# Bursts of small fp32 products split among dense matmuls in a two-layer delta-rule encoder, and the inverse placed three chunks later

## The chip, the cores and the metric

The kernel runs on one core of a Trainium2 chip. The metric is the time of one execution on the device in microseconds (us); shown are the median and the extremes of three executions. The trace is of one further execution, recorded by the hardware profiler, with its own time.

## The reference: what is computed

Two encoder layers work on 1040 tokens (1024 and 16 meta tokens) of width 1024. Per layer: RMS norm; one input projection, whose columns feed a gated delta rule in both directions (4 heads of 128) and a gated short convolution (4 groups of 128 channels); an output projection of both, added to the residual; RMS norm, a SwiGLU feed-forward, and a second residual. A last norm ends it. The part that the change touches is the delta rule, cut to its core:

```python
A = M + jnp.eye(CHUNK)                      # M strictly triangular, from keys, decay, beta
u = triangular_solve(A, vb, lower=True, unit_diagonal=True)
w = triangular_solve(A, kb * exp(G), lower=True, unit_diagonal=True)
def step(S, inp):                           # over the chunks of tokens
    v_new = u_c - w_c @ S
    o = qd_c @ S + attn_c @ v_new
    S = S * gl_c + kd_c.T @ v_new
```

It runs once forward and once backward over the tokens. The kernel solves with the inverse of A.

## The kernel before, in words

**Dense work.** `dense` (L156) is every large product. Operands are kept as a high and a low part (`whi`, `wlo` of the weights; the tiles `a`, `b` hold those of the input). For each chunk of columns (346, 346 and 348 of 1040, or 512 and 512 in the last layer's halves) and each of 8 slices of the contraction, it issues three matmuls: hi·hi (L169), hi·lo (L170), lo·hi (L171), 24 in all for a projection of 1024 rows. After each chunk's evacuation one job is taken from each of three lists, `jobs`, `jobs2`, `jobs3` (L183). An entry None lets one chunk pass.

**Order.** Engines take their instructions in the order that a scheduler writes down at build time: by priorities, and by a simulated timeline. `low(f, True)` emits a set of matmuls as one burst and ties its first to the last dense matmul emitted, so that a burst stands behind the chunk after which its job was taken. A matmul of 32x32 fp32 operands shows as two matmuls and two weight loads in the trace.

**The inverse.** The delta rule uses chunks of 128 tokens: 8 chunks by 4 heads by 2 directions gives 64 triangular matrices, 32 per direction, kept in the tiles P (`Pd[0]` forward, `Pd[1]` backward, named `P0` and `P1`). Their 32x32 diagonal blocks are inverted on VectorE by substitution (operations on `e` at L613 and `b` at L614 move blocks into matmul layout). `invert` (L606) then builds the rest from products of blocks, as jobs of the third list: `first` (L639, 128 calls of 32x32, 256 matmuls in the trace), `second_third` for each half of the matrices (L651 and L652, 96 calls, 192 matmuls), `fourth` (L675) and `fifth` (L695), 64 calls of 64x64 each, 128 matmuls. Evacuations on ScalarE and VectorE stand between the steps. The list before is seven None, then `first`, None, `second_third` twice, None, `fourth`, None, `fifth`. Products of keys and queries, `chunk_a` (L573), are jobs of the second list in the same stretch.

**The scan.** After `fifth` the scan starts: eight steps for each direction, forward and backward side by side, with products at L926 (keys or queries by state, inverse by residual, attention and keys by new values) and small ones of the meta tokens at L1004. Each step loads V (`vkd`), K (`vkd`) and the attention (`aqd`) into tile `rec`, which takes the place in SBUF of the inverse's working tile (`W` and `X`), so those loads wait until the inverse has read it for the last time. Transposes of the result are at L1071. While the scan runs, TensorE's gaps are filled with dense matmuls: the rest of the input projection, then the half of the output projection that takes the convolution's rows y (four rows; loaded at L1105, split at L1110 and L1111). The other half of it takes the delta rule's result O, split at L1138 and L1139, and can only start behind the scan.

**Places in SBUF.** The third y row (i = 2) is loaded into tile P1, the place of the backward inverse. The residual rows are loaded into `hb[0]` and `hb[1]` (L1127, eight of them), which take the places of tiles of the input projection's operand x in that layer.

All these loads are issued by SyncE (SP) in one list, in order.

## Time and profile before

| | |
|---|---|
| median of 3 executions | 2438.77 us (2432.99 to 2439.55) |
| the profiled execution's own time | 2442.37 us |
| its span, first to last instruction | 2440.6 us |
| mean granted TensorE clock | 0.995 |
| busy: PE, PEld, DVE, ACT, POOL | 2410.2, 2235.0, 1824.9, 1053.0, 68.5 us |
| inverse's matmuls, layer 0 / layer 1 | about 244 to 287 us / 1464 to 1518 us of the span |

PE is TensorE's matmuls, PEld its weight loads, which overlap them. A row of the timeline has the start, the duration, the engine, the line and the operation with its tiles and shape, a count (x), and in brackets the idle time before it with what released it; "issue" is time in which the engine waited for nothing that the profile shows. A row of a windows view gives, after the bounds and the length, the busy time and number of instructions of PE, PEld, DVE, ACT and POOL, then the granted clock of TensorE as a share of full speed, the share of DMA engines in use, and GB/s.

### The profile page before, as it was taken

What the parts mean: (1) busy time and instruction counts of PE and PEld (TensorE: products, weight loads), DVE (VectorE), ACT (ScalarE), POOL (GpSimd) and SP (SyncE); (2) the same over time, 40 slices, a digit from 0 to 9 for tenths busy, and PEclk for the clock granted to TensorE, in tenths of its full rate; (3) what the DMA queues carried; (4) which work ended last, traced back from release to release, by engine and by line L of the source; (5) the groups of instructions that cost most, each with busy time, mean ns of one, the idle gap of its engine ahead of it and who ended that gap; (6) DMA issues with size and microseconds to landing.
All of it is one profiled execution on the core that took longest, in us unless ns stands there. A gap on an engine that the chain in (4) does not pass through costs nothing.

```text
span 2440.6 us, 44951 instructions
## 1 busy us (share of the span) xinstructions
PE 2410.2 (99%) x17559; PEld 2235.0 (92%) x17559; DVE 1824.9 (75%) x3312; ACT 1053.0 (43%) x1985; POOL 68.5 (3%) x157
## 2 busy tenths in 40 slices
PE   9999899999999999999999999999999999999998
PEld 8989899999999999999999998999988888888887
DVE  6778546668888887878657885457698887878874
ACT  6652434436233433344446624345453333334444
POOL 0130000000000000000000200000000000000002
PEclk9999999999999999999999999999999999999999
DMA  4456344534222224675224553445333222347641
GB/s 135 149 160 200 108 152 149 177 111 143 101 79 101 96 79 138 215 235 160 80 90 141 175 183 127 144 148 199 123 120 109 86 104 90 122 137 248 201 132 70
DMA packets 202637, 336.60 MB, mean 138 GB/s; under 512 B 23488, under 2 KB 89208, under 8 KB 202424
## 3 DMA queue, kind: packets, MB, share of 16 engines
q1 hardware_dynamic: 174600, 295.12, 36.4%
q10 hardware_dynamic: 25648, 34.24, 4.4%
q0 software_dynamic: 2176, 4.36, 0.6%
q8 instruction: 138, 2.26, 0.4%
q14 instruction: 75, 0.61, 0.1%
HBM read 251.52 MB, written 82.12 MB: 137 GB/s over the span
## 4 chain that ended last, share of the span: by engine, by line
PE 89%; DMA 4%; DVE 3%; ACT 1%; issue 1%; SPq 0%; ACTq 0%; DVEq 0%; POOLq 0%
PE pacc L170 9%; PE pacc L169 9%; PE pacc L171 9%; PE pacc L1226 4%; PE pacc L1230 4%; PE pacc L1229 4%; PE pb L1230 3%; PE pb L1226 3%; PE pb L1229 3%; PE pf L926 3%; PE pf L1226 3%; PE pf L1230 3%; PE pf L1229 3%; PE pb L926 3%; PE pacc L1793 2%; PE pacc L1794 2%
## 5 line engine op out<-in xcount | busy, mean ns | idle before, releaser
L169 PE MATMUL pacc<-a,whi 128*128 128x346 f32 (+1 forms) x800 | 261.0, 327 | 0.7 <-ACT a L190 0.6
L171 PE MATMUL pacc<-a,wlo 128*128 128x346 f32 (+1 forms) x800 | 261.1, 327 | 0.4 <-DVE wlo L139 0.2
L171 PE MATMUL pacc<-b,wlo 128*128 128x346 f32 (+2 forms) x672 | 232.3, 346 | 1.5 <-DVE wlo L139 1.3
L169 PE MATMUL pacc<-b,whi 128*128 128x346 f32 (+2 forms) x672 | 233.2, 348 | 0.0
L170 PE MATMUL pacc<-a,whi 128*128 128x346 f32 (+1 forms) x681 | 222.8, 327 | 0.5 <-DVE a L191 0.4
L138 ACT ACTIVATE whi<-raw 128x512 fp32r<-128x512 f32 x166 | 104.5, 632 | 238.3 <-PE pacc L170 169.5
L170 PE MATMUL pacc<-b,whi 128*128 128x346 f32 (+2 forms) x580 | 200.2, 345 | 0.0
L169 PEld LDWEIGHTS pacc<-a,whi 128*128 128x128 f32 x800 | 152.2, 190 | 1.8 <-ACT a L190 1.3
L171 PEld LDWEIGHTS pacc<-a,wlo 128*128 128x128 f32 x800 | 152.0, 190 | 2.0 <-DVE wlo L139 1.1
L139 DVE TENSOR_TENSOR wlo<-raw,whi 128x512 fp32r<-128x512 f32 x166 | 113.9, 687 | 48.8 <-ACT whi L138 44.3
L171 PEld LDWEIGHTS pacc<-b,wlo 128*128 128x128 f32 x672 | 126.8, 189 | 12.1 <-DVE wlo L139 1.9
L169 PEld LDWEIGHTS pacc<-b,whi 128*128 128x128 f32 x672 | 126.8, 189 | 10.3 <-issue 1.5
L170 PEld LDWEIGHTS pacc<-a,whi 128*128 128x128 f32 x681 | 129.6, 190 | 4.9 <-issue 2.5
L170 PEld LDWEIGHTS pacc<-b,whi 128*128 128x128 f32 x580 | 109.5, 189 | 7.1 <-issue 0.6
L1208 ACT ACTIVATE whi<-rw 128x512 fp32r<-128x512 f32 (+1 forms) x84 | 51.7, 620 | 105.9 <-PE pacc L1229 28.3
L1208 ACT ACTIVATE b<-rw 128x512 fp32r<-128x512 f32 (+1 forms) x63 | 38.8, 620 | 90.2 <-PE pb L1229 35.0
L1208 ACT ACTIVATE a<-rw 128x512 fp32r<-128x512 f32 (+1 forms) x63 | 38.5, 619 | 72.0 <-PE pacc L1229 33.2
L1209 DVE TENSOR_TENSOR wlo<-rw,whi 128x512 fp32r<-128x512 f32 (+1 forms) x84 | 56.2, 672 | 6.3 <-ACT whi L1208 5.8
L333 DVE TENSOR_TENSOR a<-pacc,rstd 128x346 f32<-128x346 f32 (+2 forms) x59 | 32.6, 553 | 36.3 <-PE pacc L171 36.1
L1794 PE MATMUL pacc<-P,wlo 128*128 128x260 f32 (+1 forms) x177 | 59.4, 336 | 0.0
L1791 PE MATMUL pacc<-P,whi 128*128 128x260 f32 (+1 forms) x177 | 59.4, 336 | 0.0
L1793 PE MATMUL pacc<-P,whi 128*128 128x260 f32 (+1 forms) x177 | 59.4, 336 | 0.0
(1163 smaller groups left out, 7851.0 us busy)
## 6 DMA issues: line engine op xcount, KB each, us to landing
raw<-in_w_in SPq DMA_DIRECT2D x110, 256.0 KB, 2.9
raw<-in_w_gu SPq DMA_DIRECT2D x106, 256.0 KB, 2.6
rw<-in_w_gu SPq DMA_DIRECT2D x90, 256.0 KB, 3.1
rw<-in_w_dn SPq DMA_DIRECT2D x90, 192.0 KB, 3.4
rec<-vkd SPq DMA_DIRECT2D x61, 256.0 KB, 3.2
raw<-in_w_out SPq DMA_DIRECT2D x48, 256.0 KB, 2.8
b<-ad SPq DMA_DIRECT2D x45, 260.0 KB, 3.9
a<-ad SPq DMA_DIRECT2D x45, 256.0 KB, 2.6
```

Of the source, the lines that this page charges most:

```text
L138: whi_done[0] = hasten(wpr, lambda: act(out=hi, in_=raw[:, 0:kk, :], func=AF.Copy))
L139: whi_done[1] = hasten(wpr, lambda: tt(out=lo, in0=raw[:, 0:kk, :], in1=hi.bitcast(F32), op=ALU.subtract))
L169: mm(ps[:, :n], wh, xh[:, n0:n1], start=(i == 0), stop=False)
L170: mm(ps[:, :n], wh, xl[:, n0:n1], start=False, stop=False)
L171: last_mm[0] = mm(ps[:, :n], wl, xh[:, n0:n1], start=False, stop=(i == K - 1))
L926: one = mm(*args, **kw)
L1208: hasten(wpr, lambda: act(out=hi, in_=src, func=AF.Copy))
L1226: one = mm(ps[:, :CW], w[0][:, k, :], th[:, cs], start=first and k == 0, stop=False, skip_group_check=True)
L1229: mm(ps[:, :CW], w[0][:, k, :], tl[:, cs], start=False, stop=False, skip_group_check=True)
L1230: one = mm(ps[:, :CW], w[1][:, k, :], th[:, cs], start=False, stop=stop and k == nk - 1, skip_group_check=True)
L1793: mm(ps[:, :CW], wh[:, k, :], tl[:, cs], start=False, stop=False, skip_group_check=True)
L1794: mm(ps[:, :CW], wl[:, k, :], th[:, cs], start=False, stop=en, skip_group_check=True)
```

## The change

`first` becomes two jobs of 64 calls (128 matmuls in the trace) and each `second_third` two jobs of 48 calls (96 matmuls); PSUM banks are kept between the parts of a step, and evacuations follow the last part. So between two bursts a chunk of dense matmuls passes. The list starts with ten None instead of seven. The first job therefore comes three chunks later; the four that are added move all that follows, `fifth` and the scan among it, later still. Since P1 is then still read by the scan when the third y row is loaded, that row goes into a row of `hb[1]` in the last layer. Numbers of lines are ten higher in the changed kernel from the middle of `invert` on.

```diff
-            def first():
-                pss = [view(bank("f"), 32) for _ in halves]
+            banks_ = {}
+            def first(part):
+                if part == 0:
+                    banks_["1"] = [view(bank("f"), 32) for _ in halves]
+                pss = banks_["1"]
...
-                low(lambda: [turn(q) for q in range(16)][0][0], True)
-                act(out=QS[:, halves[0], :], in_=pss[0], func=AF.Copy, scale=-1.0)
...
+                low(lambda: [turn(q) for q in range(8 * part, 8 * part + 8)][0][0], True)
+                if part == 1:
+                    act(out=QS[:, halves[0], :], in_=pss[0], func=AF.Copy, scale=-1.0)
...
-            def second_third(qs):
-                ps2, ps3 = (view(bank(t), 32) for t in "bf")
+            def second_third(qs, part):
+                if part == 0:
+                    banks_["2"] = [view(bank(t), 32) for t in "bf"]
+                ps2, ps3 = banks_["2"]
...
-                low(lambda: [turn(q) for q in range(qs.start, qs.stop)][0][0], True)
+                low(lambda: [turn(q) for q in range(qs.start + 8 * part, qs.start + 8 * part + 8)][0][0], True)
+                if part == 0:
+                    return
...
-            return [first, None, lambda: second_third(halves[0]), lambda: second_third(halves[1]), None, fourth, None, fifth]
+            return ([lambda i=i: first(i) for i in range(2)] + [None] + [lambda qs=qs, i=i: second_third(qs, i) for qs in halves for i in range(2)]
+                    + [None, fourth, None, fifth])
...
-                jobs3.extend([None] * 7 + invert())
+                jobs3.extend([None] * 10 + invert())
...
-            t = trow() if i < 2 else big("P1")[:, 0, :] if i < 3 else y3
+            t = trow() if i < 2 else (hb[1][:, i, :] if last else big("P1")[:, 0, :]) if i < 3 else y3
```

No instruction is added or taken away on any engine; they stand in another order between the inverse and the end of the scan, in both layers. Three places show it. A row is a line, an operation, the tile written and the tiles read, and the shape (x2: two alike in a row).

The first is PE around `first` in layer 0, where `pf` is the bank of the products, `pacc` that of a dense chunk. Before:

```order
L169 MATMUL pacc_2690<-a_1_72,whi_2467 128x346
L639 MATMUL pf_2557<-e_2163,P_836 32x32 x2
L639 MATMUL pf_2558<-e_2163,P_836 32x32 x2
L170 MATMUL pacc_2690<-a_2_73,whi_2467 128x346
...
L639 MATMUL pf_2558<-e_2164,P_837 32x32 x2
L171 MATMUL pacc_2690<-a_3_74,wlo_2474 128x346
L573 MATMUL pb_2716<-b_38_213,b_39_214 128x128 x4
L169 MATMUL pacc_2746<-a_1_72,whi_2734 128x348
```

and in the changed kernel:

```order
L171 MATMUL pacc_2639<-a_3_74,wlo_2608 128x346
L643 MATMUL pf_2665<-e_2163,P_836 32x32 x2
...
L643 MATMUL pf_2666<-e_2164,P_837 32x32 x2
L171 MATMUL pacc_2731<-a_1_72,wlo_2602 128x346
L169 MATMUL pacc_2731<-a_1_72,whi_2601 128x346
...
L171 MATMUL pacc_2731<-a_3_74,wlo_2608 128x346
L643 MATMUL pf_2665<-e_2163,P_836 32x32 x2
...
L643 MATMUL pf_2666<-e_2164,P_837 32x32 x2
L169 MATMUL pacc_2839<-a_1_72,whi_2827 128x348
```

Before, four calls stand ahead, then 13 dense matmuls, then 124 calls in one stretch. In the changed kernel 64 calls, 19 dense matmuls, and 64 calls follow each other.

The second is PE at the end of the scan in layer 1, `vv` being the scan's new values and `o` the split O. Before:

```order
L169 MATMUL pacc_18714<-b_1824_18680,whi_18708 128x512
L926 MATMUL pf_17895<-vv_17892,P_14797 128x128 x4
L170 MATMUL pacc_18714<-b3f_18690,whi_18708 128x512
...
L171 MATMUL pacc_18728<-b_1824_18680,wlo_18709 128x512
L926 MATMUL pf_17895<-vv_17892,rec_17887 128x128 x4
L169 MATMUL pacc_18749<-b_1824_18680,whi_18743 128x512
```

and in the changed kernel:

```order
L171 MATMUL pacc_18937<-b_1824_18680,wlo_18918 128x512
L936 MATMUL pf_17895<-vv_17892,P_14797 128x128 x4
...
L171 MATMUL pacc_18972<-b_1824_18680,wlo_18953 128x512
L936 MATMUL pf_17895<-vv_17892,rec_17887 128x128 x4
L169 MATMUL pacc_18972<-b_1824_18680,whi_18952 128x512
...
L171 MATMUL pacc_18972<-b_1824_18680,wlo_18953 128x512
L169 MATMUL pacc_19030<-o_18986,whi_19024 128x256
```

Before, 171 dense matmuls of the y half stand between the scan's last product and the first that reads `o`; in the changed kernel six.

The third is SP's list in the same stretch, with the y rows (`yd`), the residual rows (`hd`) and the scan's loads. Before:

```order
L1105 DMA P_1829_18687<-yd_14188 128x1024
...
L1105 DMA a_1825_18681<-yd_14188 128x1024
...
L1105 DMA a_1827_18684<-yd_14188 128x1024
L916 DMA rec_17887<-aqd_14190 128x512
...
L1127 DMA b_1823_18679<-hd_206 128x1024
L1127 DMA b_1822_18678<-hd_206 128x1024 x4
L1127 DMA b_1823_18679<-hd_206 128x1024 x3
```

and in the changed kernel:

```order
L925 DMA rec_17887<-vkd_14189 128x512 x2
L926 DMA rec_17887<-aqd_14190 128x512
L1115 DMA b_1823_18679<-yd_14188 128x1024
L1137 DMA b_1822_18678<-hd_206 128x1024 x4
L1137 DMA b_1823_18679<-hd_206 128x1024 x3
...
L1137 DMA b_1823_18679<-hd_206 128x1024
L923 DMA rec_17887<-vkd_14189 128x512 x2
```

The third y row moved from the front of the three to behind them, into `hb[1]` (the tile `b_1823`); the residual rows, which before came behind the scan's last V and attention loads, now stand ahead of several of them.

## The prediction

> **What bounds the kernel now.** I read the page first, then TensorE's waits, then its timeline where those waits stand. The page says that TensorE is the bound:

> ```profile
> PE 2410.2 (99%) x17559; PEld 2235.0 (92%) x17559; DVE 1824.9 (75%) x3312; ACT 1053.0 (43%) x1985; POOL 68.5 (3%) x157
> q8 instruction: 138, 2.26, 0.4%
> ```

> The span is 2440.6 us, so PE idles for 30.4 us in all, and an edit that only moves work can gain no more than part of those, plus whatever makes its busy time too long. The view of waits of PE names those of this stretch (total, times, longest):

> ```profile
> PE pf L639 <- issue: 3.9, 2, 2.0
> PE pb L651 <- issue: 2.5, 1, 2.5
> PE pf L639 <- DVE e L613: 1.8, 3, 1.2
> ```

> Three are waits for nothing that the profile shows. The timeline puts each inside a burst of 32x32 products:

> ```profile
> 243.88 1.52 PE L639 MATMUL pf<-e,P 32*32 32x32 f32 x157 [1.19 <-DVE e L613]
> 247.37 1.10 PE L639 MATMUL pf<-e,P 32*32 32x32 f32 x91 [1.97 <-issue]
> 264.75 0.27 PE L651 MATMUL pb<-P,b 32*32 32x32 f32 x3 [2.54 <-issue]
> 1464.38 1.45 PE L639 MATMUL pf<-e,P 32*32 32x32 f32 x148 [0.43 <-DVE e L613]
> 1467.79 1.09 PE L639 MATMUL pf<-e,P 32*32 32x32 f32 x104 [1.95 <-issue]
> ```

> What are they? One view gives the number of instructions from stall to stall (PE and PEld are both PE's instructions):

> ```profile
> 247.37:264.75 17.38, 14.84 (x511) 14.20 (x511) 13.55 (x19) 8.35 (x11) 0.00 (x0) 0.90 0.27 94
> 264.75:1467.78 1203.03, 1195.13 (x9540) 1175.82 (x9539) 902.43 (x1699) 510.19 (x988) 19.45 (x51) 1.00 0.41 136
> ```

> In the first stretch 511 + 511 = 1022 instructions, with two semaphore instructions in PE's list 1024 = 4 x 256. In the page, 2 x 17559 = 35118 PE instructions meet 138 packets on the instruction queue q8, 2.26 MB or 16 KB each: one for about 254. So I read the stalls as PE out of instructions at the edge of a block of 256, its next 16 KB not yet there. Between 247.37 and 264.75 a 256-block takes 4.3 us on average; in a burst, 1.1 us for 91 calls' matmuls and loads is 182 instructions, or 1.5 us per block. Over the whole span it is 2440.6 / 138 = 17.7 us a block. A fetch that takes more than 1.5 us and less than 17.7 us is hidden in dense work, and bare in a burst that covers a whole block.

> [...]

> Behind each stall comes a second cost. Windows of 3.41 us around them, with the granted clock third from the end:

> ```profile
> 244.27:247.68 3.41, 1.44 (x162) 1.34 (x159) 3.41 (x5) 3.37 (x4) 0.00 (x0) 1.00 0.07 26
> 247.68:251.09 3.41, 3.41 (x81) 3.35 (x70) 3.07 (x5) 3.34 (x4) 0.00 (x0) 0.50 0.60 212
> 261.33:264.74 3.41, 0.88 (x105) 0.79 (x94) 0.33 (x1) 0.40 (x1) 0.00 (x0) 1.00 0.03 5
> 264.74:268.16 3.42, 3.41 (x31) 3.34 (x31) 2.75 (x4) 0.59 (x1) 0.00 (x0) 0.50 0.02 5
> 1466.24:1469.65 3.41, 1.86 (x108) 1.69 (x109) 3.41 (x7) 3.34 (x5) 0.00 (x0) 1.00 0.41 153
> 1469.65:1473.06 3.41, 3.41 (x10) 2.63 (x9) 3.21 (x6) 3.36 (x4) 0.00 (x0) 0.50 0.86 299
> 1471.27 0.63 PE L170 MATMUL pacc<-b,whi 128*128 128x512 f32 x1
> 1471.70 0.63 PE L171 MATMUL pacc<-b,wlo 128*128 128x512 f32 x1
> 1478.77 0.40 PE L171 MATMUL pacc<-b,wlo 128*128 128x512 f32 x1
> 1479.01 0.40 PE L169 MATMUL pacc<-b,whi 128*128 128x512 f32 x1
> ```

> A window with PE busy for 0.88, 1.44 or 1.86 of 3.41 us is followed by one at half clock, in which dense matmuls start 0.43 us apart instead of 0.24.

> **The change part by part.** *The stalls.* Now 128 matmuls (256 with their loads) are the longest burst of 32x32, in `first`; 96 in `second_third`. In the changed order I counted instructions in blocks of 256, taking the layer's block edges from the stalls above. The blocks that hold the first bursts have 51 or more of their 256 in dense matmuls, those of `second_third` 63 or more, and before each block stand 38 dense instructions or more. A dense matmul with its load takes 0.16 us in narrow chunks (the steps of 272.29 and 272.45 below, and 4.0 us for 25), so 24 to 48 of them are 3.8 to 7.7 us. The shorter is still longer than any of the three stalls, and the fetch has also the 1.5 us of the block's own instructions. The gain is 1.97 + 2.54 + 1.95 = 6.4 us. Bounds: 0 and 6.4, the second being taken because the nearest row, the first `second_third` burst, with dense work ahead of it, runs 192 matmuls without any stall:

> ```profile
> 254.46:256.58 2.12, 2.12 (x195) 1.85 (x193) 2.12 (x3) 0.26 (x1) 0.00 (x0) 1.00 0.60 209
> ```

> *The half-clock windows.* The loss of one is what its matmuls would have taken less at full clock. With dense matmuls of 512 columns all through it, as in the last of the three, that is 3.41 x (1 - 0.24 / 0.43) = 1.5 us. The first two also hold small products and short idle times, which the clock touches less, and I take 1.35 for each: 4.2 us together, with bounds of 0 and 4.5. I take 4.2, since a window of the changed order would hold at most two bursts of 0.8 to 1.5 us and no idle time, which is nearest to the row at 254.46 with its clock of 1.00.

> *The wait for e.* Each `first` started before VectorE had its operands: 1.8 us. It now starts three chunks later; by the orders, 54 narrow matmuls (8.6 us) later in layer 0 and 74 wide ones (17 us) in layer 1. Both exceed the longest wait, 1.2 us, so 1.8 us goes. Bounds 0 and 1.8.

> *The scan's first loads.* They wait for `fifth`, since `rec` takes the inverse's place.

> ```profile
> 292.24 1.13 PE L926 MATMUL pb<-rec,P 128*128 128x128 f32 x8 [1.41 <-DMA rec<-vkd]
> 1522.82 0.42 PE L1004 MATMUL pf<-rec,Z 16*32 16x128 f32 x8 [0.91 <-DMA rec<-vkd]
> ```

> The order has 25 narrow dense matmuls between `fifth` and the scan in layer 0, before and now: the 1.4 us stay. In layer 1 it was 25 narrow ones (4.0 us) and is now 23 of 512 columns (23 x 0.235 = 5.4 us), 1.4 us more than before and so more than 0.91: that goes. Bounds 0 and 0.9.

> *More switches.* Where other products stand between dense ones, PE loses time at the change:

> ```profile
> 272.29 0.32 PE L169 MATMUL pacc<-a,whi 128*128 128x348 f32 x1
> 272.45 0.32 PE L170 MATMUL pacc<-a,whi 128*128 128x348 f32 x1
> 272.70 0.33 PE L675 MATMUL pb<-b,P 64*64 64x64 f32 x2
> 272.95 0.43 PE L171 MATMUL pacc<-a,wlo 128*128 128x348 f32 x1
> 273.22 0.32 PE L169 MATMUL pacc<-a,whi 128*128 128x348 f32 x1
> ```

> From 272.45 to 273.22 are two dense steps, 2 x 0.16 us, and 0.45 us for one small group. The orders have 245 such places in the stretch before, 248 now: 3 x 0.45 = 1.35 us. (The splits add more; smaller scan groups that now merge take some back.)

> *The third y row.* It is loaded into x's low half, so only after the last in-projection matmul; call that T.

> ```profile
> 1692.26 1.05 PE L926 MATMUL pf<-vv,rec 128*128 128x128 f32 x8
> ad<-b SPq DMA_DIRECT2D x20, 512.0 KB, 2.7
> b<-ad SPq DMA_DIRECT2D x4, 520.0 KB, 4.6
> b<-hd SPq DMA_DIRECT2D x8, 512.0 KB, 8.4
> rec<-vkd SPq DMA_DIRECT2D x61, 256.0 KB, 3.2
> L1110 ACT ACTIVATE b<-a x6: 613/616/618, 1682.0 to 1694.3; 128x512 fp32r<-128x512 f32 x6
> ```

> On PE then come 12 matmuls of the y half that need only the first rows (12 x 0.235 = 2.8 us) and, by the order, 19 products of the scan, 38 matmuls in the trace: at 0.8 us for eight, since 0.25 of the 1.05 us overlap what follows, 3.8 us, of which I count 3.5. That is 6.3 us. The load needs 2.7 to 8.4 us to land, the split 0.62 us on ScalarE: a wait of 0 to 2.7 us. Nearest is the 4.6 us of a load of this size into the same kind of tile, so I take 0. Behind that split on ScalarE stand the scan's own copies, which PE's next scan group waits for; on SP the eight residual rows and the last loads of the scan stand behind the load. Where the row is late, those are late next.

> *The scan's end in layer 1.* Before, the last scan product, at 1692.26, stood well ahead of O's use:

> ```profile
> 1733.59 0.28 PE L169 MATMUL pacc<-o,whi 128*128 128x256 f32 x1
> L1138 ACT ACTIVATE o<-a x16: 400/402/418, 1690.6 to 1714.7; 128x256 fp32r<-128x256 f32 x16
> 1686.48 4.46 SPq L1127 DMA_DIRECT2D b<-hd  x8
> ```

> 41 us of dense work lay between; now six matmuls, 1.4 us, and the scan's steps still have about 25 wide matmuls (5.8 us) between links. O's first product needs only the middle chunks of tokens, whose last transposes stand a few steps earlier; one product of the split takes 0.40 us on ScalarE and about as long on VectorE. I cost it at 0. The cover is those 5.8 us; without it, each us by which the scan is late is a us of the total, up to the price in the third rival. In layer 0 the scan still ends 111 dense matmuls ahead, 17 us: 0.

> *Sum.* 6.4 + 4.2 + 1.8 + 0.9 - 1.35 = 11.95 us. The profiled execution took 2442.37, so it would take 2430.4. The median of the runs is 3.6 us below that execution, so I predict 2438.8 - 11.9 = 2427 us.

> **The rivals.** *The clock stays.* The stalls go, but a half-clock window comes at each change of phase anyway, as each burst of small products leaves weak activity. For: the small products all remain, and the windows quoted show a stall and a burst together, so the rows can't part the two. Against: the `second_third` burst at 254.46 has 2.12 us of small products and a granted clock of 1.00 in the window that holds it. 4.2 us less gain: 2431. [...]

> *Stalls at new places.* `fifth` in layer 0 and `fourth` in layer 1 now fill 244 and 245 of a 256-block. The nearest row is a burst of the 64x64 kind that takes 2.27 us:

> ```profile
> 284.32:286.59 2.27, 2.27 (x131) 1.99 (x129) 1.46 (x3) 1.97 (x3) 0.00 (x0) 1.00 0.37 116
> ```

> If a fetch starts only as the block before it is entered and takes 3.4 to 3.9 us (2.5 us of stall and 1.1 to 1.5 us of burst), each stalls for 1.1 to 1.6 us, and a half-clock window of 1.3 us may follow: 5 to 6 us back, 2433. Against: 84 or more dense instructions stand ahead of each.

> *The scan's end is late: slower.* On SP nine loads of 512 KB (the third y row and the residual rows) now wait for T, and the V loads of the scan's next steps stand behind them. By the order, 105 wide matmuls of the y half stand between T and the product that needs that V: 105 x 0.235 = 24.7 us. If the nine go together as in the row above, V lands 4.46 + 8.4 us behind T, and its own 3.2 us after these: 16 us, in time. If they go one behind the other at the 2.7 or the 4.6 us of the single rows, that is 24 or 41 us, and 27 or 45 with V: PE waits 3 to 20 us, and since the y half runs out with the scan, all of it goes to the end. 2427 + 20 = 2447. The change turns slower from where V lands 19 us behind its need, 44 us behind T. For: the eight are issued in 4.46 us and share the same engines. Against: in the same row they land after 8.4 us, not eight times that of one.

> *It doesn't do it.* The order shows dense matmuls between all bursts, so the split is real; but if the stalls are no fetches, they come again, at 2438 to 2440.

> **How the numbers follow.** The forecast has 0.58, the clock 0.17, new stalls 0.10, the late end 0.08, no effect 0.07. A change under 0.3% (7.3 us) is about what this kernel's measurement can't tell from none, so faster means below 2431.5. That holds for 0.9 of the forecast, half of the clock's case and a fifth of the new stalls: 0.52 + 0.09 + 0.02 = 0.63. Slower means above 2446: 0.06, most of it the late end. The rest, 0.31, is no difference. The likeliest's own range is 2422 to 2432 (all terms at the ends nearest to them, and the spread of the runs); for 8 in 10 I take 2420 to 2438, which holds the first three cases.

> **What would show it.** Right: no idle time released by issue within L643, L658 or L659; a granted clock of 1.00 in all windows of the inverse; no wait for e at `first`; the wait for `rec` left only in layer 0; PE running without a gap from T through the first product that reads `o`. Wrong: idle time of 1 us or more inside `fourth` or `fifth`; half-clock windows behind a burst with no stall; PE waiting for the third y row, for `rec` or for `o` in layer 1's tail. More than 19 us of such waits there would make it slower.

## The result, and the profile after

The changed kernel took 2427.06 us (median of four, 2424.01 to 2428.56) against 2438.2 (four, 2432.99 to 2439.55): a ratio of 0.9957, 95% interval 0.9939 to 0.9975. Run again later, beside three other kernels on one chip, it took 2428.47 us (five) against 2441.14 (nine): 0.9944, 0.9931 to 0.9958. The forecast was 2427. That the number was met so closely is partly luck, as the terms below show: two were wrong in opposite directions.

The busy times on the page of the profile after:

```profile
PE 2403.6 (99%) x17559; PEld 2227.7 (92%) x17559; DVE 1823.3 (75%) x3312; ACT 1054.4 (43%) x1985; POOL 68.2 (3%) x157
```

and its waits of PE (total, times, longest):

```profile
PE pacc L169 <- DVE b L870: 2.1, 1, 2.1
...
PE pb L573 <- DVE dt L577: 0.8, 1, 0.8
...
PE pb L936 <- DMA rec<-vkd: 0.2, 1, 0.2
```

There is as much to do as before, in 2426.3 us of span instead of 2440.6. The waits for issue, for e, and nearly all for `rec` are gone; a wait of 2.1 us for an evacuation on VectorE (L870 is L860 of before) is new. To see where the time came from, the two stages that the change touches are cut out by counting dense matmuls: from the 1000th to the 2250th that starts, and from the 4000th to the 5250th. Before:

```profile
212.13:516.51 304.38, 296.69 (x2908) 291.52 (x2906) 187.54 (x399) 116.22 (x316) 0.00 (x0) 0.99 0.46 155
1447.33:1764.11 316.78, 313.46 (x2837) 289.18 (x2837) 200.41 (x399) 129.42 (x329) 0.00 (x0) 0.99 0.48 156
```

and after:

```profile
208.97:505.51 296.54, 294.21 (x2906) 288.57 (x2906) 187.64 (x400) 115.96 (x316) 0.00 (x0) 1.00 0.48 159
1436.47:1750.60 314.13, 312.87 (x2839) 287.83 (x2838) 199.41 (x398) 130.42 (x329) 0.00 (x0) 1.00 0.47 156
```

Layer 0's stage is 7.8 us shorter, layer 1's 2.7: 10.5 of the 14.3 us between the two spans. The other 3.8 us lie outside the stages, most of them where the two kernels have the same work in the same order. The profiled execution of before had half-clock windows (3.41 us with a granted clock of 0.50) at 56.5 and 138.5 us and the one of after had none there, so nothing shows these 3.8 us to be a gain of the change.

The bursts themselves, in a windows view of after (`first` twice, one part of `second_third`, `fourth` and `fifth` of layer 1, then each layer's whole inverse):

```profile
250.73:252.02 1.29, 1.29 (x130) 1.25 (x129) 1.13 (x2) 0.00 (x0) 0.00 (x0) 1.00 0.00 0
255.14:256.43 1.29, 1.29 (x130) 1.25 (x129) 1.29 (x2) 0.66 (x2) 0.00 (x0) 1.00 0.00 2
264.18:265.20 1.02, 1.02 (x98) 0.98 (x97) 0.52 (x1) 0.00 (x0) 0.00 (x0) 1.00 0.00 0
1515.44:1517.54 2.10, 2.10 (x130) 2.03 (x129) 0.52 (x1) 0.88 (x2) 0.00 (x0) 1.00 0.00 0
1527.03:1529.12 2.09, 2.09 (x130) 2.02 (x129) 0.97 (x2) 0.88 (x2) 0.00 (x0) 1.00 0.03 8
244.00:330.00 86.00, 85.80 (x1382) 82.23 (x1383) 45.65 (x76) 34.19 (x65) 0.00 (x0) 1.00 0.35 117
1455.00:1540.00 85.00, 83.74 (x1273) 72.39 (x1272) 47.19 (x67) 30.25 (x48) 0.00 (x0) 1.00 0.33 112
```

PE is busy through each burst, and the granted clock is 1.00 through both inverses.

### The profile page after: what moved, and what is told of

Its sections match the earlier page's. It is cut to its first block, busy times and chain, and to the rows that moved or that the text cites. A ratio compares the mean times of both kernels' runs of the same rounds, so it can differ in the third digit from the quotient of the medians.

```text
span 2426.3 us, 44950 instructions
## 1 busy us (share of the span) xinstructions
PE 2403.6 (99%) x17559; PEld 2227.7 (92%) x17559; DVE 1823.3 (75%) x3312; ACT 1054.4 (43%) x1985; POOL 68.2 (3%) x157
## 3 DMA queue, kind: packets, MB, share of 16 engines
q8 instruction: 138, 2.26, 0.4%
## 4 chain that ended last, share of the span: by engine, by line
PE 90%; DMA 4%; DVE 4%; ACT 1%; issue 1%; ACTq 0%; SPq 0%; DVEq 0%; POOLq 0%
PE pacc L169 9%; PE pacc L170 9%; PE pacc L171 9%; PE pacc L1236 4%; PE pacc L1240 4%; PE pacc L1239 4%; PE pb L1240 3%; PE pb L1236 3%; PE pb L1239 3%; PE pf L936 3%; PE pb L936 3%; PE pf L1236 3%; PE pf L1240 3%; PE pf L1239 3%; PE pacc L1804 2%; PE pacc L1803 2%
## 5 line engine op out<-in xcount | busy, mean ns | idle before, releaser
L169 PE MATMUL pacc<-a,whi 128*128 128x346 f32 (+1 forms) x800 | 259.7, 325 | 2.5 <-DVE b L870 2.1
L171 PE MATMUL pacc<-a,wlo 128*128 128x346 f32 (+1 forms) x800 | 259.0, 325 | 0.0
L169 PE MATMUL pacc<-b,whi 128*128 128x346 f32 (+2 forms) x672 | 233.6, 348 | 0.5 <-DVE a L870 0.5
L171 PE MATMUL pacc<-b,wlo 128*128 128x346 f32 (+2 forms) x672 | 231.4, 345 | 1.8 <-DVE wlo L139 1.7
L170 PE MATMUL pacc<-a,whi 128*128 128x346 f32 (+1 forms) x681 | 221.3, 325 | 0.4 <-DVE a L191 0.4
L170 PE MATMUL pacc<-b,whi 128*128 128x346 f32 (+2 forms) x580 | 199.2, 344 | 0.0
L169 PEld LDWEIGHTS pacc<-a,whi 128*128 128x128 f32 x800 | 150.8, 189 | 3.9 <-DVE b L870 2.4
L171 PEld LDWEIGHTS pacc<-a,wlo 128*128 128x128 f32 x800 | 150.4, 188 | 1.3 <-issue 0.9
L171 PEld LDWEIGHTS pacc<-b,wlo 128*128 128x128 f32 x672 | 126.4, 188 | 12.1 <-DVE wlo L139 2.3
L169 PEld LDWEIGHTS pacc<-b,whi 128*128 128x128 f32 x672 | 126.4, 188 | 10.8 <-issue 1.5
L170 PEld LDWEIGHTS pacc<-a,whi 128*128 128x128 f32 x681 | 128.2, 188 | 4.4 <-issue 2.3
L170 PEld LDWEIGHTS pacc<-b,whi 128*128 128x128 f32 x580 | 109.1, 188 | 7.0 <-issue 0.7
L333 DVE TENSOR_TENSOR a<-pacc,rstd 128x346 f32<-128x346 f32 (+2 forms) x59 | 32.6, 553 | 39.7 <-PE pacc L171 39.6
## 6 DMA issues: line engine op xcount, KB each, us to landing
raw<-in_w_in SPq DMA_DIRECT2D x110, 256.0 KB, 2.8
raw<-in_w_gu SPq DMA_DIRECT2D x106, 256.0 KB, 2.8
rw<-in_w_gu SPq DMA_DIRECT2D x90, 256.0 KB, 2.8
rec<-vkd SPq DMA_DIRECT2D x61, 256.0 KB, 3.2
raw<-in_w_out SPq DMA_DIRECT2D x48, 256.0 KB, 2.9
a<-ad SPq DMA_DIRECT2D x45, 256.0 KB, 3.4
```

What stands on the lines that cost most here:

```text
L169: mm(ps[:, :n], wh, xh[:, n0:n1], start=(i == 0), stop=False)
L170: mm(ps[:, :n], wh, xl[:, n0:n1], start=False, stop=False)
L171: last_mm[0] = mm(ps[:, :n], wl, xh[:, n0:n1], start=False, stop=(i == K - 1))
```

## The experiments

For each kernel the table gives its median beside that of before in the same comparison, the ratio with its interval, and the two stages in its profile, cut by the count of dense matmuls as above.

| kernel | us, of before | ratio (95%) | layer 0, layer 1 stage, us |
|---|---|---|---|
| before, profiled | | | 304.4, 316.8 |
| the change, profiled first | 2427.1, 2438.2 | 0.9957 (0.9939 to 0.9975) | 296.5, 314.1 |
| split only | 2434.9, 2439.7 | 0.9977 (0.9967 to 0.9987) | 299.7, 313.8 |
| late only | 2442.1, 2439.7 | 1.0007 (0.9995 to 1.0019) | 303.2, 316.5 |
| late only, again | 2441.9, one execution | | 302.2, 319.3 |
| before + 128 instructions | 2453.3, 2439.7 | 1.0054 (1.0039 to 1.0069) | 307.3, 322.5 |
| before + 28 instructions | 2434.5, 2439.1 | 0.9975 (0.9965 to 0.9985) | 306.7, 313.8 |
| nine None | 2429.9, 2441.1 | 0.9953 (0.9939 to 0.9966) | 296.0, 315.9 |
| the change again | 2428.5, 2441.1 | 0.9944 (0.9931 to 0.9958) | 297.0, 315.4 |
| eleven None | 2432.0, 2441.1 | 0.9962 (0.9949 to 0.9976) | 296.5, 316.6 |
| thirteen None | 2443.1, 2439.1 | 1.0013 (1.0004 to 1.0022) | 305.0, 319.8 |
| third y row in P1 | 2439.5, 2439.1 | 1.0002 (0.9993 to 1.0012) | 295.1, 326.7 |
| moves spread | 2425.3, 2439.7 | 0.9944 (0.9926 to 0.9963) | 297.5, 313.5 |
| moves spread, again | 2426.9, 2441.1 | 0.9940 (0.9927 to 0.9952) | 295.9, 313.8 |

### Are the stalls fetches of blocks of instructions?

The late start with whole bursts, from the kernel before:

```diff
-                jobs3.extend([None] * 7 + invert())
+                jobs3.extend([None] * 13 + invert())
...
-            t = trow() if i < 2 else big("P1")[:, 0, :] if i < 3 else y3
+            t = trow() if i < 2 else (hb[1][:, i, :] if last else big("P1")[:, 0, :]) if i < 3 else y3
```

> The bursts are whole as before, but the list starts with thirteen None, so the scan starts where it does in the change, and the third y row goes into the other tile as there. Fetch theory: three stalls again, at the new edges of the blocks of 256: in layer 0's first step with some 93 products left, in the second burst of layer 0's second step with some 38 left (1 to 1.5 us), in layer 1's first step with 1 or 2 of 256 products left; the first and third 1.9 to 2.1 us. Half-clock windows follow at least two of them. Issue waits 5 to 6 us, time 2433 to 2437. Rival (a burst runs out at a fixed count, which before was 157, 171 and 152 products into the burst): in layer 1 the stall comes at about 152 products again, not at 254. Second rival (the late start removes the stalls): no issue waits, 2427.

Its timeline of PE:

```profile
263.00 0.99 PE L639 MATMUL pf<-e,P 32*32 32x32 f32 x93 [2.09 <-issue]
281.02 0.18 PE L652 MATMUL pf<-b,P 32*32 32x32 f32 x1 [2.02 <-issue]
1498.50 0.21 PE L639 MATMUL pf<-e,P 32*32 32x32 f32 x1 [2.01 <-issue]
1514.81 0.21 PE L652 MATMUL pf<-a,P 32*32 32x32 f32 x1 [0.76 <-issue]
```

Three stalls of 2.0 to 2.1 us, with 93, 38 and 1 products left in their bursts (38 by count from the row at 281.02): each at the expected instruction, the second longer than the 1 to 1.5 us expected. In layer 1 the stall came after 255 products, where before it came after 152, so a burst doesn't run out at a count. The fourth, 0.76 us, was not expected. Nor was the time: 2442.1 us, where 2433 to 2437 was expected.

A harder case leaves the bursts whole and pushes the program along. (The scheduler also put products between 75 and 221 us of layer 0 in another order, in this kernel and the next, and in the next single dense matmuls in layer 1's scan.)

```diff
-            mm(psG[:, 72:144], ones, fl(g), start=True, stop=True)
+            for _ in range(33 if l == 0 else 1):
+                mm(psG[:, 72:144], ones, fl(g), start=True, stop=True)
```

> The kernel before with one product of 128 by 72 columns, early in layer 0, issued 33 times instead of once (the result is the same): 128 instructions more on TensorE's list, nothing else moved, so all block edges stand 128 instructions earlier in the program behind it. Fetch theory: the stalls move. Layer 0's first step stalls with some 33 products left (91 before); in the second step the stall moves from its second burst (21 left) to its first, at the very end of it (the block holds 252 small ones and the last 4 instructions are dense); layer 1's first step stalls with some 40 left (104 before), and its second step, which had none, stalls in the first burst with some 33 left; a fifth of 0.5 us may follow in its second burst. Each 1.9 to 2.5 us, 8 us in all against 6.4. The repeats take 3 to 6 us where they stand. Time 2441 to 2448. Rival (the stall belongs to the burst, by its length or its data): the same three places with the same counts, 6.4 us, 2441 to 2444.

Its timeline of PE:

```profile
71.43 7.57 PE L430 MATMUL pb<-g,ones 128*128 128x72 f32 x66
253.59 0.36 PE L640 MATMUL pf<-e,P 32*32 32x32 f32 x32 [1.98 <-issue]
264.54 0.45 PE L169 MATMUL pacc<-a,whi 128*128 128x346 f32 x1 [2.13 <-issue]
1475.31 0.56 PE L640 MATMUL pf<-e,P 32*32 32x32 f32 x41 [2.27 <-issue]
1493.28 0.27 PE L652 MATMUL pb<-P,a 32*32 32x32 f32 x3 [2.18 <-issue]
```

The first row is the repeated product, the others are the stalls. They moved to the named places: 32 left (33 expected); two dense matmuls behind a burst; 41 left (40); and a burst that had never stalled now did, with 33 left by count. A fifth of 0.58 us stood at 1504.9, as expected too. They are 9.1 us in all against 6.5. With the 7.1 us of repeats that makes 2449.4; the kernel took 2453.3, and its profile shows half-clock windows behind four of these stalls and two in a row behind a wait for `rec`, three more than before had there, which at the 1.35 us each of the prediction, an estimate, would be the rest. The size was missed (2441 to 2448 expected), the places were not.

The same with 8 repeats asks whether a good place of the edges alone, with work added and nothing split, makes the kernel faster:

```diff
-            mm(psG[:, 72:144], ones, fl(g), start=True, stop=True)
+            for _ in range(8 if l == 0 else 1):
+                mm(psG[:, 72:144], ones, fl(g), start=True, stop=True)
```

> The kernel before with that same early product of layer 0 issued 8 times instead of once: 28 instructions more on TensorE's list, 1.6 us of them (64 matmuls took 7.1 us in the run with 33), no burst split, nothing moved. By the block theory, with a fetch that must cover 3.9 to 4.4 us from 64 instructions ahead of a block to its end, this place of the edges leaves one stall instead of three: in the second burst of layer 0's second step with 35 products left, 1.6 to 2.2 us; under 0.5 us in layer 0's first step (some 108 left) and behind layer 1's first. Issue waits 1.6 to 3 us against 6.4; with fewer half-clock windows and the 1.6 us of repeats 2433 to 2437, faster than before although work was added. Rival (a burst of 192 or 256 stalls by itself): three stalls, 6 us or more, 2440 to 2443.

Its timeline of PE:

```profile
244.38 1.37 PE L640 MATMUL pf<-e,P 32*32 32x32 f32 x108 [2.37 <-issue]
262.00 0.23 PE L652 MATMUL pb<-P,b 32*32 32x32 f32 x4 [2.31 <-issue]
1487.02 0.23 PE L652 MATMUL pb<-P,a 32*32 32x32 f32 x4 [0.43 <-issue]
```

It was faster by 0.25% with 28 instructions more. Layer 1's stall of 1.95 us is gone, and its stage is 3.0 us shorter; the one of the second step stands where it was expected. But layer 0's `first` stalled for 2.4 us with 108 products left, where under 0.5 was expected, and layer 0's stage is 2.3 us longer. The place of that stall is right and its size wrong: I had let a fetch start 64 instructions ahead of a block, which here would have counted the 13 dense matmuls ahead of the burst. The 64 was an assumption that no run shows, and the 3.9 to 4.4 us an estimate (at the second stall of before the 320 instructions up to the one that was waited for, all inside the burst, took 4.1 us). So its profile doesn't explain the 4.7 us between the medians: the two stages are 0.7 us shorter together, and 4.0 of the 5.6 us between the two spans lie ahead of the 1000th dense matmul (208.2 us against 212.1), in the stretch with another order, where before has two half-clock windows and this kernel one. That the places of the edges made this kernel faster is not shown.

In six profiles with 18 stalls over 0.7 us, the instruction 256 ahead of the one that was waited for started 3.2 to 3.9 us earlier. The trace also has the fetches themselves, as packets of the instruction queue q8. Around the second stall of before almost nothing else moved, so a windows view shows them (0.1 us at 165 GB/s are 16 KB; a packet's bytes are put down to its start):

```profile
261.80:261.90 0.10, 0.10 (x35) 0.10 (x24) 0.00 (x0) 0.00 (x0) 0.00 (x0) 1.00 0.93 165
261.90:264.75 2.85, 0.31 (x37) 0.21 (x24) 0.00 (x0) 0.00 (x0) 0.00 (x0) 1.00 0.00 0
265.85:265.95 0.10, 0.10 (x2) 0.10 (x2) 0.07 (x2) 0.01 (x1) 0.00 (x0) 0.50 0.59 164
```

PE entered the block ahead at 260.94; the packet started 0.9 us later and took 1.47 us; PE ran dry at 262.2 and went on at 264.75, 1.4 us after the packet's end. It is the same at all 23 stalls of 0.3 us or more, in seven profiles: PE goes on 1.2 to 1.5 us after the end of a packet, and the instruction it goes on with has the same place in a block of 256, counted from PE's first (remainder 193, weight loads and semaphore instructions included). This shows that the stalls are fetches. Two more bursts of before would stall if each fetch started only when PE enters the block ahead; their packets started 1.4 and 2.2 us before that, and in every profile half of all packets or more start over 1.5 us before it (58% before, 61% after). What makes a packet start early or late stays open.

### Is it the split or the later place?

```diff
-                jobs3.extend([None] * 10 + invert())
+                jobs3.extend([None] * 7 + invert())
```

> The bursts are split as in the change, but the list starts with seven None as before, so the inverse begins where it began before. Theory (stalls are fetches of blocks of 256 instructions; a half-clock window follows a stall; the later start only serves the operands): the two stalls inside the second step's bursts and in layer 1's first are gone; in layer 0 the order puts only 2 dense matmuls and one group of keys by queries between the two halves of the first step, so a block there has 238 of 256 instructions in small products, and a stall of 0.5 to 1.3 us may remain. TensorE waits for e again, 1 to 2 us. Time 2428 to 2433 us. Rival (the later start does it): stalls and half-clock windows stay as before, 5 us or more of issue waits, time 2436 to 2440.

What its timeline of PE has of waits in the inverse:

```profile
245.40 1.04 PE L643 MATMUL pf<-e,P 32*32 32x32 f32 x100 [0.82 <-issue]
1461.78 1.25 PE L643 MATMUL pf<-e,P 32*32 32x32 f32 x124 [0.54 <-DVE e L613]
```

One stall of 0.82 us is left, in the block where the order had only two dense matmuls between the parts, as expected; the others are gone. The wait for e is 0.5 us, where 1 to 2 was expected. The split alone makes the kernel 0.23% faster, less than expected. Layer 1's stage is as short as in the change. Layer 0's is 3.2 us longer: beside the stall, PE waits 0.7 us for `rec`, 1.1 for the scan's `qs`, and 2.4 for additions of the residual on VectorE (L1125). That accounts for less than half of the 6 to 8 us by which the medians of split only and of the change differ; the rest lies outside the two stages of that one profile (half-clock windows at 9.7 and 57.5 us, and 0.8 us of waiting behind the scan) and wasn't settled.

The late start alone gains nothing: its stalls stayed, the wait for e went, and 0.9 us for an evacuation (L333), 0.8 for `dt`, 1.1 and 0.9 in the scan came. The two parts together give more than their sum (-4.7 and +2.4 us against -11.1 and -12.7 in two comparisons). The medians show that; the profiles explain only the part in layer 0.

### What follows a stall: the half clock

The late start with whole bursts ran ten times between 2436.5 and 2445.0 us, and its profile had been the fastest. So a second profile was taken, of the same kernel.

> The late start with whole bursts a second time, for a second profile: its ten runs lay between 2436.5 and 2445.0 us with a median of 2442, above the 2433 to 2437 expected, while the profiled one, at 2436.5, was the fastest. Theory (it is the half-clock windows: the three stalls are always there, in the first profile only one window followed them): the same three stalls with the same counts of products left, and two or more half-clock windows; each costs up to 1.7 us. Rival (another wait comes and goes, in the scan's tail): a wait of 2 us or more there that the first profile lacks.

Its timeline of PE:

```profile
265.56 0.99 PE L639 MATMUL pf<-e,P 32*32 32x32 f32 x93 [2.01 <-issue]
284.94 0.18 PE L652 MATMUL pf<-b,P 32*32 32x32 f32 x1 [1.86 <-issue]
1501.13 0.21 PE L639 MATMUL pf<-e,P 32*32 32x32 f32 x1 [2.66 <-issue]
```

and windows of 3.41 us around the first and the third (the granted clock is third from the end):

```profile
263.20:266.62 3.42, 1.41 (x135) 1.27 (x123) 0.00 (x0) 0.10 (x1) 0.00 (x0) 1.00 0.00 0
266.62:270.03 3.41, 3.41 (x13) 3.41 (x14) 0.00 (x0) 1.85 (x4) 0.00 (x0) 0.51 0.02 5
1498.60:1502.02 3.42, 0.89 (x6) 0.85 (x7) 0.21 (x1) 1.08 (x3) 0.00 (x0) 1.00 0.59 231
1502.02:1505.43 3.41, 3.41 (x14) 3.41 (x14) 0.00 (x0) 0.57 (x1) 0.00 (x0) 0.55 0.02 5
```

The same instructions stall, and half-clock windows follow the first and the third. In the first profile of the same kernel the only one in the inverses followed the second; the windows around its second and its first stall:

```profile
278.65:282.06 3.41, 1.39 (x82) 1.23 (x70) 0.51 (x1) 0.00 (x0) 0.00 (x0) 1.00 0.02 5
282.06:285.47 3.41, 3.41 (x13) 3.41 (x13) 2.24 (x4) 1.62 (x3) 0.00 (x0) 0.50 0.02 5
261.58:264.99 3.41, 1.99 (x100) 1.95 (x100) 0.00 (x0) 1.01 (x2) 0.00 (x0) 1.00 0.02 5
264.99:268.40 3.41, 3.41 (x23) 3.41 (x23) 1.06 (x2) 1.93 (x4) 0.00 (x0) 1.00 0.06 8
```

The half-clock windows in the profile of before start at 56.53, 138.45, 247.68, 264.74 and 1469.65 us, a whole number of 3.413 us apart (24, 32, 5 and 353). In these rows a stall of 2.0 to 2.7 us that fell into one such window left PE busy for 0.89 to 1.41 us of it, and the next had a granted clock of 0.50 to 0.55; the first stall of the first profile straddled two, left 1.99 us in the second, and cost nothing more. So these six stalls cost 1.9 to 2.7 us each, and some of them a half-clock window more, up to 1.5 us by the prediction's estimate from matmuls 0.43 instead of 0.24 us apart. A wait was followed by one too: in the kernel with 28 instructions more a half-clock window came at 291.1, behind a wait of 2.1 us for `rec`.

PE's busy time in a window doesn't decide alone. Early in layer 0 the second profile has a window with 2.69 us busy (51.68 to 55.09) that is followed by two at half clock, the first profile one with 2.62 us (51.35 to 54.77) that is followed by full clock; in the profile of before 2.65 us (53.12 to 56.53) is followed by half clock and 2.58 us (128.21 to 131.63) by full. What else counts isn't shown. These two windows more, at the estimate of 1.35 us, and the one more in the inverses are 4 of the 5.4 us between the two profiled executions. They don't explain the median of 2442: the ten executions had a granted clock of 0.995 to 0.998, those of before beside them, at a median of 2439.7, 0.993 to 0.997. What slows that kernel stays open.

### Where the later place stops paying

> The changed kernel with nine None, one chunk earlier. By the order layer 1 has 16 dense matmuls of 512 columns between the scan's last product and the first that reads o, against six, and a block of 256 in layer 0's first step that may stall 0.5 to 0.8 us. Theory (at ten the tail costs nothing, so an earlier start wins nothing there): 2426 to 2430 us. Rival (ten is already too late somewhere): 2422 to 2425.

> The changed kernel with eleven None, one chunk later. By the order no dense matmul of 512 columns is left between the scan's last product and the first that reads o. Theory (the tail's slack ends about here; thirteen cost 16 us): waits of 0 to 3 us for vv or o in layer 1's tail, and one of 0 to 2 us in layer 0's scan, 2428 to 2434. Rival (the loss comes only with the thirteenth): 2425 to 2428.

> The changed kernel with thirteen None instead of ten: bursts split as there, all inverse steps and the scan three more chunks later. By the order no dense matmul of the output projection's y half is then left for the scan's last step in layer 1: 20, 4 and 8 products follow each other there, with the links over VectorE and ScalarE bare. Theory (the change's place ends just short of the point where the scan's end sets the time): TensorE waits 3 to 8 us in all in layer 1's tail for vv, qs, a3f or o, nothing new elsewhere: 2430 to 2435. Rival (there is slack left, O's first half covers the chain): no wait above 1 us there, 2425 to 2428.

All three change only the number of None (nine, eleven, thirteen). With nine, a block in layer 0's `first` stalls for 0.48 us with 25 products left, where the order had a block with little dense work; 2429.9 us, as expected, within the interval of the change. With eleven, PE waits where the scan ends in layer 1:

```profile
1720.15 0.63 PE L1081 MATMUL pa<-ident,a3f 128*128 128x128 f32 x4 [0.68 <-ACT vv L973]
1722.20 0.39 PE L170 MATMUL pacc<-o,whi 128*128 128x256 f32 x1 [0.28 <-DVE o L1149]
```

(both from PE's timeline) and the kernel takes 2432.0, 3.5 us more than the change beside it. The intervals of the two overlap, and the two waits are 1.0 us, so how much the eleventh costs isn't settled. With thirteen it takes 2443, far above the 2430 to 2435 expected. The scan's end in layer 1 has the waits that were expected, but smaller (four of 0.34 to 0.69 us, 1.9 in all where 3 to 8 was expected, the last before `o`), and more is lost in layer 0, of which the expectation said nothing. From its timeline of PE:

```profile
317.36 1.16 PE L936 MATMUL pb<-rec,P 128*128 128x128 f32 x8 [1.16 <-DVE P L715]
471.38 0.81 PE L169 MATMUL pacc<-a,whi 128*128 128x348 f32 x2 [2.29 <-ACT a L1120]
1731.25 1.16 PE L936 MATMUL pf<-vv,rec 128*128 128x128 f32 x8 [0.69 <-ACT vv L973]
1733.16 0.39 PE L170 MATMUL pacc<-o,whi 128*128 128x256 f32 x1 [0.51 <-DVE o L1149]
```

The scan there starts before VectorE has stored the inverse (L715), and the split of the y rows (L1120) stands on ScalarE in one list with the scan's copies: PE waits 2.3 us for it. Half-clock windows follow both waits (at 319.0 and 472.6 us). Layer 0's stage is 8.5 us longer than in the change, layer 1's 5.7. So both layers bound the place between ten and thirteen; nine and ten can't be told apart.

### The third y row

```diff
-            t = trow() if i < 2 else (hb[1][:, i, :] if last else big("P1")[:, 0, :]) if i < 3 else y3
+            t = trow() if i < 2 else big("P1")[:, 0, :] if i < 3 else y3
```

> The changed kernel with the third y row put back into tile P1, the backward inverse. That row then waits for the scan's last product with the backward inverse, and the y half of the output projection for the row. By the order some 60 products of the scan then stand with no dense work between them. Theory (the other tile is what lets the late scan be covered): TensorE waits 10 to 25 us in layer 1's scan, for links of the scan over VectorE and ScalarE; 2437 to 2450. Rival (other dense work fills it): within 3 us of the change, 2425 to 2430.

The two longest waits in its timeline of PE:

```profile
1670.44 2.07 PE L936 MATMUL pb<-S,a 128*128 128x128 f32 x8 [4.48 <-DVE a3f L1071]
1680.68 1.16 PE L936 MATMUL pb<-vv,rec 128*128 128x128 f32 x8 [2.36 <-ACT vv L973]
```

The scan stands bare, and layer 1's stage is 12.6 us longer: the whole gain of the change. The waits are 8.3 us, fewer than expected. Two half-clock windows follow the longest, from 1669.1 to 1676.0 us, in which 16 products take 3.62 us, against 1.95 at full clock (at 1681.67), and 8 take 2.07, against 1.16: some 2.7 us more.

### Can the new wait be taken away?

The wait of 2.1 us for L870 has this cause, in VectorE's timeline of the changed kernel:

```profile
235.74 2.22 DVE L613 STREAM_TRANSPOSE e<-b 128x1024 f32<-128x1024 f32 x1
237.86 1.98 DVE L614 STREAM_TRANSPOSE b<-b 128x1024 f32<-128x1024 f32 x1
239.70 2.06 DVE L613 STREAM_TRANSPOSE e<-b 128x1024 f32<-128x1024 f32 x1
241.60 1.94 DVE L614 STREAM_TRANSPOSE b<-b 128x1024 f32<-128x1024 f32 x1
243.35 0.54 DVE L870 TENSOR_TENSOR b<-pacc,b 128x346 f32<-128x346 f32 x1
```

and PE's row:

```profile
243.96 0.43 PE L169 MATMUL pacc<-a,whi 128*128 128x346 f32 x1 [2.13 <-DVE b L870]
```

Four moves of 2 us stand in a row, the evacuation of a dense chunk behind them, and PE waits for its end. Before, the same four ran, and PE waited for the third of them at `first`. The experiment makes them jobs of the third list, each tied to the end of another chunk:

```diff
-                nc.vector.transpose(out=XB[d].rearrange("p q c -> p c q"), in_=cols)
+                    after(nc.vector.transpose(out=XB[d].rearrange("p q c -> p c q"), in_=cols), ends_[-1])
...
+            return ([lambda d=d, z=z: blocks(d, z) for d in range(2) for z in range(2)] + [corners] + [lambda i=i: first(i) for i in range(2)] + [None] + [lambda qs=qs, i=i: second_third(qs, i) for qs in halves for i in range(2)]
...
-                jobs3.extend([None] * 10 + invert())
+                jobs3.extend([None] * 5 + invert())
```

> The changed kernel, with the four moves of the inverted blocks on VectorE (2 us each, one behind the other) tied each to the end of another dense chunk, five chunks ahead of the first step and on, so that evacuations of dense chunks stand between them on VectorE. Theory (in the change the wait for e is gone, but a wait of 2.1 us of a dense matmul for an evacuation that stands behind these four, and 0.5 and 0.8 us in layer 1, took its place): these go, 2 to 3.4 us, with no new wait above 0.5 us; 2424 to 2426. Rival (VectorE is full there; what isn't late at one place is late at another): the same waits elsewhere, or e late again, 2426 to 2429.

> The spread moves on VectorE again, beside the changed kernel on the same chip. Theory (one wait of 2 us was traded for another of 1.9 us, for ScalarE's split of the weights): within 0.1% of the changed kernel. Rival (layer 1's 1.3 us and lesser ones are won): 1 to 2.5 us faster than it.

The row of PE nearest to that place, in its first profile:

```profile
247.19 0.43 PE L169 MATMUL pacc<-a,whi 128*128 128x348 f32 x1 [1.89 <-ACT whi L138]
```

The wait for L870 went, and in this execution one of 1.9 us for a split of weights on ScalarE came; in the second it was 0.5 us. The medians are 2425.3 and 2426.9 against 2427.1 and 2428.5 of the change, 1.6 to 1.8 us less, both within the intervals: perhaps a gain, too small to be told.

The changed kernel was run beside it.

> The changed kernel itself once more, on the chip of the next three: 2425 to 2429 us, no wait for issue above 0.3 us inside the inverse, no half-clock window there. If a window does come there without a stall, the theory that they follow the stalls is wrong.

No half-clock window stood in its inverses, and no wait for issue above 0.3 us.

## Why the prediction was right

The sum was 11.95 us; the two stages of the profiles give 10.5. Term by term:

- **The stalls, 6.4 us: right.** All three are gone, and their cause, which was only argued, is shown: the two pushed kernels move their places with the count of instructions, and each ends right behind the packet of a block. The cover is thinner than I counted: in the profile after, the fullest blocks of `first` have 38, 44 and 50 dense instructions, where I counted 51 or more, and most of those of `second_third` 48, where I counted 63. In the thinnest (251.6 to 255.9 us) the next block was needed 1.9 us after the end of its packet, where stalls show 1.2 to 1.5; split only and nine None stalled inside `first` in layer 0, for 0.82 and 0.48 us. Of the 138 fetches of before PE waited for three, each inside a burst of small products, for 1.95 to 2.54 us; no other wait for issue stands in its view of PE's waits.
- **The half-clock windows, 4.2 us: right for this execution, but no constant.** All three are gone. Here they followed stalls, and in the late start not the same stalls in its two profiles; the first rival falls, since no half-clock window stood in the inverses of the two profiles of the change and the two of the spread moves, which have all the bursts and no stall. The price of 4.2 us was not measured by itself: the rows show it together with the switches, below. The granted clock fell to 0.50 after windows of 3.41 us with 0.88 to 1.86 us of work in the inverses of before, and early in its layer 0 after one with 2.65; one with 2.02 us in the profile after (242.56 to 245.97) was followed by a clock of 1.00.
- **The wait for e, 1.8 us: wrong.** It went, but the step "both exceed the longest wait, so 1.8 us goes" asked only whether `first` would wait. VectorE's four moves take 8 us at both places (8.1 in layer 0 before, 8.2 after), and with PE no longer waiting for them at `first`, others wait behind them: two dense matmuls for evacuations, 2.13 and 0.48 us, and a product of keys for `dt`, 0.79 us, 3.4 in all. The term is -1.6, not +1.8.
- **The scan's first loads, 0.9 us: too small.** I kept the 1.4 us in layer 0, since the order had 25 dense matmuls there in both. In the profile after, 0.2 us of `rec` waits are left, so 2.5 went; in the one that was taken later 0.7 us stood there. The count on PE's list bounds when the load is needed, not when SP gets to it: before, SP issued the first of these loads 0.9 us after `fifth`'s last product, behind a store (`szd`), and in the profile after 0.1 us after it.
- **The switches, 1.35 us: about right.** PE's busy time in the two stages, in the rows above, fell by 2.5 and 0.6 us, 3.1 together; 4.2 for the clock less 1.35 for the switches is 2.85. Only this difference is measured: if the clock's share is 4.2, the switches cost 1.1. Together 6.4 + 4.2 + 1.8 - 3.4 + 2.5 - 1.1 = 10.4.
- **The third y row at 0: right.** Its load landed in 5.1 us (4.6 was taken), and PE did not wait. **The scan's end at 0: right, with little to spare** (with eleven None PE waits there). From the load's issue at T to the first product that reads `o` PE was busy without a gap. The load's row among the DMA issues, and the window:

```profile
b<-yd SPq DMA_DIRECT2D x1, 512.0 KB, 5.1
```

```profile
1651.95:1719.63 67.68, 67.68 (x402) 59.09 (x400) 49.02 (x115) 30.50 (x107) 0.00 (x0) 1.00 0.55 184
```

Of the rivals, stalls at new places did not come: `fifth` with 244 and `fourth` with 245 of a block's 256 ran through, 2.1 us each. The slower one did not come at ten. At thirteen the kernel was slower than before, but from another side: not late loads of V behind the residual rows but the links of the scan and the split of the y rows on ScalarE.

## What to carry to other kernels

Idle time that is put down to nothing, inside a run of very small matmuls, is worth a count of instructions: here two stalls stood 1024 instructions apart, four packets' worth of 256; the change, with dense work between the bursts, had none of the three that took 6.4 us before; and 128 or 28 instructions more elsewhere moved stalls or removed one. So compare kernels by their stalls before believing an unrelated edit. A wait that is taken away at one consumer of a busy engine can return at the next one, as here 1.8 us for `e` came back as 3.4 us of other waits for VectorE: ask what that engine's list holds behind the work that was waited for. Where work is placed later to hide it, try one step more and one less; here three chunks more cost 15 us, and one more 3.5, at the edge of what these runs can tell.
